# A hybrid decoder layer: the z product in token groups of 272/256/512 columns, splits moved from GpSimd to VectorE, and the residual's added row moved to w_out's token tiles

## The chip, the core and the metric

The kernel runs on one core of a Trainium2 chip. A core has five engines with queues of their own: TensorE (PE in the profile; PEld is its weight loads), VectorE (DVE), ScalarE (ACT), GpSimd (POOL) and SyncE (SP), which here only starts transfers. Each works through its queue in order. The metric is the device time of one execution in microseconds; the time of before is the median of three runs. A profile is of one more execution, whose span runs from its first to its last instruction.

## The reference

One layer over 1040 tokens (16 meta tokens and 1024 of the sequence), 1024 wide:

```
h = layer_norm(concat(meta, x), in_ln_g, in_ln_b)
z = h @ w_in + b_in                     # 3840 columns: q 512 | k 128 | v 128 | conv 2 x 512 | gates 2 x 1024
a = swa_sink_attention(q, k, v, ...)    # window 128, 16 meta keys, sinks, relative bias
c = silu(layer_norm(causal_dwconv(c_val * sigmoid(c_gate), 31 taps)))
mixed = sigmoid(g_attn) * (a @ w_attn_proj) + sigmoid(g_conv) * (c @ w_conv_proj)
h = layer_norm(alpha * h + mixed @ w_out)
f = (gelu(g) * u) @ ffn_w_down          # u, g = causal_dwconv(h @ ffn_w_up, 3 taps)
out = layer_norm(alpha * h + f)         # without the meta tokens
```

The first h, before the layer, is `xn * in_ln_g + in_ln_b` with xn the centred and scaled row. So the residual alpha * h is `xn * (alpha * in_ln_g) + alpha * in_ln_b`: a row that is multiplied and a row that is added.

## The kernel before

**Products.** Every large product is done with operands split in two: a float32 value is a high part (rounded by ACT, `nc.scalar.copy`) and a low part (the difference). A product of one 128-row chunk is three matmuls, high x high, high x low, low x high, the third with the low weights. `product` (line 297) issues them: lines 301, 305 and 306. The helper `split` (line 272) makes the two parts of a weight tile; its subtraction runs on DVE when `quick` is set and on POOL otherwise (line 276).

**Stages in order of time.** (1) The input stage to 56 us: rows of x are normed, transposed on PE, scaled and split into `h0`, the layer's input by channel, and the first tiles of z (k, v and q's first quarter) are formed at once, three tiles by three token groups `HG`, at lines 514 and 517. (2) The z product, to 416 us: 27 more tiles of 128 columns of `w_in` (8 of the convolution's input, 3 of q, 16 gates), each over all tokens. A tile is 8 chunks x 3 token groups x 3 matmuls, 72 in all. The conv tiles take the groups `ZG`, 400/384/256 columns, the q and gate tiles `TG`, the same without the first 14 tokens, 386/384/256. Attention (lines 740 to 873) runs in between, its matmuls among the gates'. DVE meanwhile runs the convolution, 31 taps for each of four channel chunks (line 669). Behind it, `csum` adds the four chunks for the LayerNorm over channels (lines 884 to 888), whose DVE work is pinned in order (`cln_*`), followed by the splits of attention's output (`o_split`, lines 985 to 991). (3) The projections of both branches, 416 to 505 us, eight tiles of `w_ab` (line 1079), merged with the gates that come back from DRAM (`merge`, line 1089). (4) w_out, 505 to 609 us, nine token tiles in the order 3, -1, 7, 2, 6, 0, 4, 1, 5 (`out_rows`, line 1228; -1 is the two meta rows that are kept). A tile loads its residual row from `h0d`, adds the product's two halves, norms and is transposed for the next stage during the next tile's product. (5) The up product with its convolution and gate, 609 to 1039 us (line 1497), and (6) the down product to the end (line 1635), both by a Strassen-like scheme of seven products on sums of quadrants.

**Where h0 lies.** Two buffers of 8320 columns, `RHO` and `RHC`, hold the eight chunks of h0, high and low. `h0(k, hl, a, b)` (line 255) gives columns a to b: part i = 2 (k mod 4) + hl begins at column 1040 i, so a matmul on the high part and the one on the low part read places 1040 columns apart. In the up product the quadrant sums (`bsum`, line 1154) lie four blocks of 256 or 258 columns apart, high to low, and one block from chunk to chunk; in the down product operands are blocks of 512 columns with the low part 1024 further.

**Weights.** `weights` (line 281) counts its calls: 1 to 3 are the input stage's, 4 to 30 z's, 31 to 38 the projections'. Up to the 23rd the split is on DVE, from the 24th on POOL. `pair_of` gives one of two buffers for each of the high and low parts; the low one begins 16 columns into its buffer.

**Evacuation.** A group's sum lies in one of three PSUM banks (`tag="mm", bufs=3`). ACT reads it into one of five buffers of 400 columns (`stage`, line 328). For a gate it is stored to `sgd` from ACT's queue (line 677); for q it is split and stored and loaded (`q_evac`).

**The residual** (line 438): the two rows of the input LayerNorm are loaded for all partitions, scaled by alpha, and DVE multiplies and adds them to the nine tiles of xn (line 450) behind the split of the fourth and the fifth weights; the result is stored to `h0d`.

**The order of work.** A planner orders each engine's instructions by rank (`rank`, a lower number first: `RK_TURN` 450, `RK_SPLIT` 500, `RK_EVAC` 600, and so on) and by its own timing. `after` pins one instruction behind another; in w_out, `line` (line 1166) makes one fixed order of DVE's work for tiles 0, 4, 1 and 5, in which the sums for the up product and the first splits of its weights stand between the tiles' own steps.

Of the kernel before, what the change touches and what calls it, by code (L numbers as in the profile page):

```python
# [29 lines left out]
P = 128  # L30
# [21 lines left out]

ZG = [(0, 400), (400, 784), (784, 1040)]

# [47 lines left out]
def tile_hybrid_layer(  # L102
# [152 lines left out]
    def h0(k, hl, a, b):  # L255
        o = ((k % 4) * 2 + hl) * T
        return (RHO if k < 4 else RHC)[:, o + a:o + b]
# [22 lines left out]

    def weights(shape, fill):
        fills[0] += 1
        n = fills[0]
        own = n == 3
        raw = sp.tile(shape, F, name="wr3") if own else wraw(shape)
        with rank({1: 13, 2: 18, 3: 17, 4: 23}.get(n, RK_SPLIT)):
            last_fill.append(fill(raw))
        hi, lo = (sp.tile(shape, R, name=t + "3") for t in ("whi", "wlo")) if own else pair_of("whi", "wlo", 16, shape)
        if n <= 3:
            return hi, lo, raw  # L290
        with rank(RK_SPLIT):
            last_split.append(split(raw, hi, lo, n <= 23))
        return hi, lo
# [31 lines left out]

    st_next = [0]

    def stage(n, lo=4104, cnt=5):
        i = st_next[0] % cnt
        st_next[0] += 1  # L330
        return FA[:, lo + i * 400:lo + i * 400 + n]

# [17 lines left out]
    def q_evac(r):  # L350
        def evac(g, a, b, ps):
            t = stage(b - a)
            nc.scalar.activation(t, ps, AF.Identity, bias=qb[:, r:r + 1], scale=HD ** -0.5)
            h, l = (qsp.tile([P, 400], R, name=n, tag=n)[:, :b - a] for n in ("qsh", "qsl"))
            nc.scalar.copy(h, t)
            nc.vector.tensor_tensor(l, t, f32(h), OP.subtract)
            for hl, (put, x) in enumerate(((store, f32(h)), (load, f32(l)))):
                c = 0
                if g == 0:
                    c = P + 2  # L360
                    put(qd[:, (hl * 4 + r) * c:(hl * 4 + r + 1) * c], x[:, :c])
                n = (b - a - c) // P
                if n == 0:
                    continue
                i = (a - U0 + c) // P
                put(dram(qd, q_at(i) + (hl * 4 + r) * P, [[8 * U, P], [8 * P, n], [1, P]]),
                    x[:, c:].rearrange("p (n q) -> p n q", q=P))
        return evac
# [69 lines left out]
    def residual(n, *js):  # L438

        if not gb:  # L440
            for i in range(2):
                gb.append(sp.tile([P, D], F, name="gb", tag="x", bufs=8))
                with rank(24):
                    load(gb[i], dram(ln0_in, i * D, [[0, P], [1, D]]))
            for t in gb:
                after(nc.vector.tensor_scalar(t, t, ALPHA, None, OP.mult), first_nm)
        for j in js:
            t, lo = (xns[j], 0) if j >= 0 else (xm, 96)
            for op, t2 in zip((OP.mult, OP.add), gb):
                after(nc.vector.tensor_tensor(t[lo:], t[lo:], t2[lo:], op), last_split[n])  # L450
            load(*((h0d[2 + j * P:2 + (j + 1) * P, :], t) if j >= 0 else (h0d[0:2, :], xm[96 + U0:96 + NMETA])))
# [171 lines left out]
    att = ExitStack()  # L623
    cp = att.enter_context(tc.tile_pool(name="cin", bufs=2, side="right", reuse_waits="tile"))
    ap = att.enter_context(tc.tile_pool(name="att", bufs=1, side="right", reuse_waits="tile"))

# [115 lines left out]
    gate_tile(0)  # L742
    ahead = chunks_done[first_chunk + KC + 5]

# [132 lines left out]
    for o in order:  # L877
# [4 lines left out]
        if o == "c3":  # L882

            csum = cp.tile([P, 16 + T], F, name="csum", tag="cin")[:, :U]
            with rank(RK_EVAC):
                nc.gpsimd.tensor_tensor(csum, acc[0], acc[1], OP.add)
                nc.gpsimd.tensor_tensor(csum, csum, acc[2], OP.add)
                nc.vector.tensor_tensor(csum, csum, acc[3], OP.add)
# [127 lines left out]
    for g in range(3):  # L1016
# [7 lines left out]
    wo_stack = ExitStack()  # L1024
    RW = wo_stack.enter_context(tc.tile_pool(name="rw", bufs=1, side="right", reuse_waits="tile")).tile(
        [P, 2048], R, name="RW")
    RT = OB[:, 0:2048]
# [50 lines left out]
    for m in range(KC):  # L1078
        hi, lo = weights([P, KC, P], lambda raw: load(raw, w_ab[m]))

# [32 lines left out]
        else:  # L1113
            pa = [branch(0, g, "mm", 3) if g < 3 else branch(0, g, "s", 2) for g in range(4)]
            for g in range(4):
                last_gate, last_act = merge(g, pa[g], branch(1, g, "t", 2))
        if m in (2, 3):
            raw = (FA[:, 4112:5136], OB[:, 3072:4096])[m - 2]
# [109 lines left out]
    def out_rows(i, between=(), work=()):  # L1228
# [13 lines left out]
        st = small.tile([P, 2, 6], F, name="st")  # L1242
        pin = line if i in (0, 4, 1, 5) else lambda ins: ins
        for half in range(2):
            hs = slice(half * 512, half * 512 + 512)
# [19 lines left out]
        if n < P:  # L1265
            q = FA[:4, 0:1024]
            load(q[0:2], h0d[0:2, :])
            nc.vector.tensor_tensor(r, r, q[0:2], OP.add)
            load(q[0:2], whole[2:4])
            nc.vector.tensor_tensor(r, r, q[0:2], OP.add)  # L1270
# [519 lines left out]
```

## Time and profile before

| what | us |
|---|---|
| median of three runs (1259.07 to 1259.88) | 1259.1 |
| the profiled execution's own time | 1259.33 |
| its span | 1257.1 |
| DVE L450, the residual's 18 multiplications and additions | 21.2 |
| POOL L276, all 19 splits on POOL | 47.5 |
| POOL L886 and L887, the two adds of csum | 4.0 |
| matmuls of z on PE by line and half (L301, L305, L306; `RHO`, `RHC`), six groups of 324 | 103.4 to 104.7 each, busy |

PE's granted clock was 0.998 of full speed. A row of a group view reads: line, engine, operation, output <- inputs, shape and count, then busy time and the mean of one in ns, then how long the engine sat idle before them and what ended it. A row of the timeline reads: start, duration (both us), engine, line, operation, operands, count; in brackets, the idle time before it and what released it. Matmuls are pipelined, so their durations overlap and the distance of their starts is what they cost. A row of the windows reads: the stretch, its length, and for each engine its busy time and count.

### The profile page before, as it was taken

The numbers are of one execution on the slowest core, as the hardware profiler recorded it, in microseconds if no ns is written. First come the engines' busy times: TensorE is split into PE (matmuls) and PEld (weight loads), VectorE is DVE, ScalarE is ACT, GpSimd is POOL, SyncE is SP. The second block draws the span as 40 slices with busy tenths as digits, with TensorE's granted clock in tenths as the row PEclk, the third lists the DMA queues.
The fourth block names the chain that finished last, engine by engine and source line by source line (L and its number), as shares of the span: only waits on it lengthen the run. The fifth ranks groups of instructions, "written<-read, shape, count | busy, mean of one in ns | idle before, by whom it ended". The sixth has DMA issues, their size and how long they took to land.

```text
span 1257.1 us, 21713 instructions
## 1 busy us (share of the span) xinstructions
PE 1246.0 (99%) x8546; PEld 1179.2 (94%) x8546; DVE 1086.6 (86%) x1859; ACT 587.4 (47%) x1057; POOL 54.1 (4%) x28
## 2 busy tenths in 40 slices
PE   9999999999999999999999999999999999999997
PEld 8999999999999999788899999999999998888886
DVE  7899989999989587648899999999999986995697
ACT  7522244545474222335565555554555554544330
POOL 0000000010112132000000000000000000000000
PEclk9999999999999999999999999999999999999999
DMA  7294733332155565222145555463464568998722
GB/s 279 73 309 104 192 95 97 106 94 81 68 141 178 155 171 140 77 75 101 68 134 185 193 210 187 184 218 117 154 230 164 203 211 318 390 328 298 249 86 84
DMA packets 96152, 212.10 MB, mean 169 GB/s; under 512 B 10787, under 2 KB 35939, under 8 KB 95922
## 3 DMA queue, kind: packets, MB, share of 16 engines
q1 hardware_dynamic: 84282, 199.64, 47.4%
q10 hardware_dynamic: 11768, 11.08, 2.7%
q8 instruction: 67, 1.10, 0.4%
q14 instruction: 35, 0.29, 0.1%
HBM read 150.29 MB, written 62.70 MB: 169 GB/s over the span
## 4 chain that ended last, share of the span: by engine, by line
PE 96%; ACT 1%; DVE 1%; DMA 0%; issue 0%; ACTq 0%; DVEq 0%; SPq 0%
PE px L1497 14%; PE py L1497 9%; PE ps_x L1635 9%; PE ps_z L305 8%; PE ps_z L301 8%; PE ps_z L306 8%; PE ps_z L1635 7%; PE pz L1497 5%; PE pw L1497 5%; PE ps_p L306 2%; PE ps_p L301 2%; PE ps_p L305 2%; PE ps_w L306 2%; PE ps_w L301 2%; PE ps_w L305 2%; PE ps_z L517 2%
## 5 line engine op out<-in xcount | busy, mean ns | idle before, releaser
L669 DVE SCALAR_TENSOR_TENSOR FA<-cin,cols,FA 128x1026 f32<-128x1026 f32 x120 | 155.2, 1305 | 0.2
L301 PE MATMUL ps_z<-RHO,whi 128*128 128x384 f32 (+2 forms) x324 | 104.7, 323 | 0.2 <-ACT FA L676 0.2
L305 PE MATMUL ps_z<-RHC,whi 128*128 128x384 f32 (+2 forms) x324 | 104.5, 323 | 0.0
L305 PE MATMUL ps_z<-RHO,whi 128*128 128x384 f32 (+2 forms) x324 | 104.0, 321 | 0.0
L306 PE MATMUL ps_z<-RHC,wlo 128*128 128x384 f32 (+2 forms) x324 | 103.7, 320 | 0.0
L301 PE MATMUL ps_z<-RHC,whi 128*128 128x384 f32 (+2 forms) x324 | 103.7, 320 | 0.0
L306 PE MATMUL ps_z<-RHO,wlo 128*128 128x384 f32 (+2 forms) x324 | 103.4, 319 | 0.0
L1316 DVE TENSOR_TENSOR RHO<-wr,RHO 128x512 fp32r<-128x512 f32 x94 | 63.6, 686 | 5.4 <-ACT RHO L1315 5.4
L1315 ACT CAST RHO<-wr 128x512 fp32r<-128x512 f32 x94 | 56.7, 620 | 24.4 <-DVE wr L1333 11.5
L273 ACT CAST whi<-wr 128x1024 fp32r<-128x1024 f32 x37 | 38.9, 1051 | 56.3 <-PE ps_z L305 31.9
L301 PEld LDWEIGHTS ps_z<-RHO,whi 128*128 128x128 f32 x324 | 60.9, 188 | 0.9 <-ACT FA L676 0.4
L305 PEld LDWEIGHTS ps_z<-RHC,whi 128*128 128x128 f32 x324 | 60.9, 188 | 0.4
L306 PEld LDWEIGHTS ps_z<-RHC,wlo 128*128 128x128 f32 x324 | 60.9, 188 | 0.2
L301 PEld LDWEIGHTS ps_z<-RHC,whi 128*128 128x128 f32 x324 | 60.9, 188 | 0.2
L306 PEld LDWEIGHTS ps_z<-RHO,wlo 128*128 128x128 f32 x324 | 61.0, 188 | 0.1
L305 PEld LDWEIGHTS ps_z<-RHO,whi 128*128 128x128 f32 x324 | 60.9, 188 | 0.1
L1333 DVE TENSOR_TENSOR wr<-wr 128x512 f32<-128x512 f32 x88 | 60.3, 685 | 0.2
L276 POOL TENSOR_TENSOR wlo<-wr,whi 128x1024 fp32r<-128x1024 f32 x17 | 42.3, 2488 | 185.3 <-ACT whi L273 175.7
L676 ACT ACTIVATE FA<-ps_z,cols 128x386 f32<-128x386 f32 (+2 forms) x48 | 26.0, 541 | 46.6 <-PE ps_z L306 39.1
L1509 ACT COPY FA<-px 128x514 f32<-128x514 f32 (+2 forms) x23 | 13.1, 571 | 68.0 <-PE px L1497 67.8
L1316 DVE TENSOR_TENSOR ws<-wr,ws 128x512 fp32r<-128x512 f32 x60 | 40.6, 686 | 4.5 <-ACT ws L1315 4.3
L1422 ACT ACTIVATE FA<-OB,cols 128x512 f32<-128x512 f32 x44 | 35.9, 816 | 14.0 <-DVE OB L1505 14.0
(467 smaller groups left out, 3567.3 us busy)
## 6 DMA issues: line engine op xcount, KB each, us to landing
wr<-in_w_up_dram SPq DMA_DIRECT2D x44, 512.0 KB, 4.6
wr<-in_w_z_dram SPq DMA_DIRECT2D x30, 512.0 KB, 4.0
fd<-FA SPq DMA_DIRECT2D x44, 256.0 KB, 2.5
OB<-in_w_down_dram SPq DMA_DIRECT2D x19, 512.0 KB, 6.2
qt<-qd SPq DMA_DIRECT2D x28, 256.0 KB, 3.7
td<-OB SPq DMA_DIRECT2D x12, 512.0 KB
sums<-fd SPq DMA_DIRECT2D x12, 512.0 KB, 4.8
sd<-sums SPq DMA_DIRECT2D x12, 512.0 KB, 2.7
```

The costliest lines, as they stand in the source:

```text
L273: ins = nc.scalar.copy(hi, raw)
L276: return (nc.vector if quick else nc.gpsimd).tensor_tensor(lo, raw, f32(hi), OP.subtract)
L301: ins = nc.tensor.matmul(ps, ah, bh, start=i == 0, stop=False)
L305: nc.tensor.matmul(ps, ah, bl, start=False, stop=False)
L306: last = nc.tensor.matmul(ps, al, bh, start=False, stop=i == n - 1)
L669: nc.vector.scalar_tensor_tensor(acc[c], cin[:, j:j + U], wc, acc[c], OP.mult, OP.add)
L1315: nc.scalar.copy(hi, src)
L1316: ins = nc.vector.tensor_tensor(lo, src, f32(hi), OP.subtract)
L1333: ins = nc.vector.tensor_tensor(*x)
L1422: nc.scalar.activation(t, cc[:, 2:HW], AF.Identity, bias=ffw(3, o), scale=ffw(2, o))
L1497: ins = nc.tensor.matmul(o, x[:, ks], bmat(sub, q, hl, k), start=first and k + j == 0, stop=k == 3 and j == 2, skip_group_check=not first)
L1635: nc.tensor.matmul(banks[i], l[:, ts], r[:, ws], start=first and a and x + k == 0, stop=z and x == len(ops) - 1 and k == 2, skip_group_che ...
```

## The change

Four edits are made together.

1. The token groups of z become 272/256/512 (258/256/512 for q and gates). h0's parts are laid out anew: the first 272 columns of the parts lie 272 columns apart behind column 6144 (those of the first part at 0), the other 768 columns lie 768 apart from column 272 on. The evacuation buffers become three of 272 and two of 512 columns. The anchor behind which attention begins, a chunk of the first gate tile, moves with the groups.
2. Where `weights` splits, the subtraction is always on DVE; csum's first two adds are on DVE. The splits of w_out's fourth to seventh chunk stay on POOL.
3. The low weights' offset of 16 columns is kept for the projections alone; z's begin at 0.
4. The residual stage only multiplies. The added row, alpha * in_ln_b, is loaded during the second tile of the projections, scaled by alpha at the fourth, and added to each tile of w_out before its product. A small pad moves attention's tiles by 8 columns.

```diff
-ZG = [(0, 400), (400, 784), (784, 1040)]
+ZG = [(0, 272), (272, 528), (528, 1040)]
...
     def h0(k, hl, a, b):
-        o = ((k % 4) * 2 + hl) * T
+        i = (k % 4) * 2 + hl
+        if a < 272:
+            o = i * 272 + (6144 if i else 0)
+        else:
+            o = i * 768
         return (RHO if k < 4 else RHC)[:, o + a:o + b]
...
-    def weights(shape, fill):
+    def weights(shape, fill, shift=0):
...
-        hi, lo = (...) if own else pair_of("whi", "wlo", 16, shape)
+        hi, lo = (...) if own else pair_of("whi", "wlo", shift, shape)
         if n <= 3:
             return hi, lo, raw
         with rank(RK_SPLIT):
-            last_split.append(split(raw, hi, lo, n <= 23))
+            last_split.append(split(raw, hi, lo, True))
...
-    st_next = [0]
-
-    def stage(n, lo=4104, cnt=5):
-        i = st_next[0] % cnt
-        st_next[0] += 1
-        return FA[:, lo + i * 400:lo + i * 400 + n]
+    st_next = [0, 0]
+
+    def stage(n):
+        big = n > 272
+        i = st_next[big] % (2 if big else 3)
+        st_next[big] += 1
+        o = 4136 + (816 + i * 512 if big else i * 272)
+        return FA[:, o:o + n]
...
         if not gb:
-            for i in range(2):
-                gb.append(sp.tile([P, D], F, name="gb", tag="x", bufs=8))
-                with rank(24):
-                    load(gb[i], dram(ln0_in, i * D, [[0, P], [1, D]]))
+            gb.append(sp.tile([P, D], F, name="gb", tag="x", bufs=8))
+            with rank(24):
+                load(gb[0], dram(ln0_in, 0, [[0, P], [1, D]]))
...
-            for op, t2 in zip((OP.mult, OP.add), gb):
-                after(nc.vector.tensor_tensor(t[lo:], t[lo:], t2[lo:], op), last_split[n])
+            after(nc.vector.tensor_tensor(t[lo:], t[lo:], gb[0][lo:], OP.mult), last_split[n])
...
+    cp.tile([P, 8], F, name="pad_i", tag="pad", bufs=1)
...
-    ahead = chunks_done[first_chunk + KC + 5]
+    ahead = chunks_done[first_chunk + 2 * KC + 2]
...
-                nc.gpsimd.tensor_tensor(csum, acc[0], acc[1], OP.add)
-                nc.gpsimd.tensor_tensor(csum, csum, acc[2], OP.add)
+                nc.vector.tensor_tensor(csum, acc[0], acc[1], OP.add)
+                nc.vector.tensor_tensor(csum, csum, acc[2], OP.add)
...
+    beta = rw_p.tile([P, D], F, name="beta")
...
-        hi, lo = weights([P, KC, P], lambda raw: load(raw, w_ab[m]))
+        hi, lo = weights([P, KC, P], lambda raw: load(raw, w_ab[m]), 16)
...
+        if m == 1:
+            load(beta, dram(ln0_in, D, [[0, P], [1, D]]))
+        if m == 3:
+            with rank(RK_EVAC):
+                nc.vector.tensor_scalar(beta, beta, ALPHA, None, OP.mult)
...
         pin = line if i in (0, 4, 1, 5) else lambda ins: ins
+        if n == P:
+            with rank(RK_TURN):
+                pin(nc.vector.tensor_tensor(r, r, beta, OP.add))
...
             nc.vector.tensor_tensor(r, r, q[0:2], OP.add)
+            nc.vector.tensor_tensor(r, r, beta[0:2], OP.add)
```

More of the change, by code (lines that the diff above doesn't have):

```diff
@@ L287, in weights @@
             last_fill.append(fill(raw))
-        hi, lo = (sp.tile(shape, R, name=t + "3") for t in ("whi", "wlo")) if own else pair_of("whi", "wlo", 16, shape)
+        hi, lo = (sp.tile(shape, R, name=t + "3") for t in ("whi", "wlo")) if own else pair_of("whi", "wlo", shift, shape)
         if n <= 3:
@@ L353, in evac @@
             nc.scalar.activation(t, ps, AF.Identity, bias=qb[:, r:r + 1], scale=HD ** -0.5)
-            h, l = (qsp.tile([P, 400], R, name=n, tag=n)[:, :b - a] for n in ("qsh", "qsl"))
+            h, l = (qsp.tile([P, 512], R, name=n, tag=n)[:, :b - a] for n in ("qsh", "qsl"))
             nc.scalar.copy(h, t)
@@ L1024, in tile_hybrid_layer @@
     wo_stack = ExitStack()
[L1025 to L1026 removed]
+    rw_p = wo_stack.enter_context(tc.tile_pool(name="rw", bufs=1, side="right", reuse_waits="tile"))
+    RW = rw_p.tile([P, 2048], R, name="RW")
+    beta = rw_p.tile([P, D], F, name="beta")
     RT = OB[:, 0:2048]
```

## The prediction

> **What bounds the kernel now.** I read the page's busy times first, then the waits of TensorE, then its timeline.
>
> ```profile
> span 1257.1 us, 21713 instructions
> PE 1246.0 (99%) x8546; PEld 1179.2 (94%) x8546; DVE 1086.6 (86%) x1859; ACT 587.4 (47%) x1057; POOL 54.1 (4%) x28
> ```
>
> TensorE (PE) has work in 1246.0 of 1257.1 us. Who it waited for, from the view of its waits (us in total, times, longest):
>
> ```profile
> PE ps_w L541 <- DVE ones_r L222: 1.1, 1, 1.1
> PE pw L1497 <- ACT FA L1298: 1.0, 1, 1.0
> PE ps_z L301 <- ACT FA L676: 0.2, 1, 0.2
> ```
>
> These are the two longest, and the only one in the z product behind the input stage. So no edit can gain much by ending a wait; time falls only if PE's matmuls stand closer together, and rises if a slower engine makes PE wait. How close they stand is read from starts in the timeline (start, us, engine, line), not from durations, because matmuls overlap. The rows that begin each group of 24 matmuls, for one tile of the convolution's input (groups 400/384/256) and one gate tile (386/384/256), with the first row behind:
>
> ```profile
> 67.89 0.34 PE L301 MATMUL ps_z<-RHO,whi 128*128 128x400 f32 x1
> 72.23 0.34 PE L301 MATMUL ps_z<-RHO,whi 128*128 128x384 f32 x1
> 76.45 0.28 PE L301 MATMUL ps_z<-RHO,whi 128*128 128x256 f32 x1
> 79.28 0.34 PE L301 MATMUL ps_z<-RHO,whi 128*128 128x400 f32 x1
> ...
> 405.17 0.34 PE L301 MATMUL ps_z<-RHO,whi 128*128 128x386 f32 x1
> 409.44 0.34 PE L301 MATMUL ps_z<-RHO,whi 128*128 128x384 f32 x1
> 413.65 0.28 PE L301 MATMUL ps_z<-RHO,whi 128*128 128x256 f32 x1
> 416.48 0.28 PE L301 MATMUL ps_p<-OA,whi 128*128 128x258 f32 x1
> ```
>
> The conv tile takes 11.39 us, the gate tile 11.31: per matmul 181 ns at 400 columns, 178 at 386, 175 at 384, 118 at 256. Other stages show what a matmul can cost:
>
> ```profile
> 609.05 1.58 PE L1497 MATMUL px<-OC,RHO 128*128 128x256 f32 x12
> 610.46 1.58 PE L1497 MATMUL pz<-OC,RHO 128*128 128x256 f32 x12
> ...
> 631.95 1.60 PE L1497 MATMUL px<-RHC,ws 128*128 128x258 f32 x12
> 633.39 1.52 PE L1497 MATMUL px<-OC,ws 128*128 128x256 f32 x12
> 634.75 1.59 PE L1497 MATMUL pz<-RHO 128*128 128x258 f32 x12
> ...
> 1044.95 5.60 PE L1635 MATMUL ps_z<-OC,RX 128*128 128x512 f32 x24
> 1050.39 5.60 PE L1635 MATMUL ps_z<-OC,RHC 128*128 128x512 f32 x24
> ```
>
> 512 columns: 5.44 us for 24, 226.7 ns each. 256 columns at 633.39: 1.36 us for 12, 113.3 ns, the same 0.443 ns per column. 258 columns: 120 ns, some 5.6 more than 0.443 x 258. At 0.443 the z groups would be 177, 171, 170 and 113.4: each stands 4 to 7 ns too far apart. In the code the operands of the rows without this extra follow each other in steps of whole 256 columns (256 and 1024 in the up product, 512 and 1024 in the last one); with it are steps of 258 there and of 1040 in z. The row at 609.05 speaks against the step as the only cause: the same 256-column operands, 117.5 ns.
>
> **The change part by part.**
>
> *The z groups.* The columns and the matmuls stay (27 tiles of 72 on this path). The 256 and 512 groups now read parts 768 columns apart, three times 256; the first group, 258 or 272, reads parts 272 apart. A gate or q tile (19 of them) becomes 24 x (120 + 113.3 + 226.7) = 11.04 us, against 11.31: 0.27 less. If 256 stays at 117.5, it is 11.14: 0.17 less. 272 has no clean row; 120 x 272/258 = 126.5 makes a conv tile (8) 11.20 to 11.30 against 11.39: 0.19 to 0.09 less. Sum: 19 x 0.27 + 8 x 0.19 = 6.6 us, or 19 x 0.17 + 8 x 0.09 = 3.9. I take 6.2, near the upper figure, since the 256 group follows a 258 or 272 group, as at 633.39; a part of the tiles is cut up by attention and counts for less. Lower end: the extra belongs to every matmul in z whatever its step; three per term then stay three, gain 0. Upper end: 258 and 272 lose theirs too, 24 x 5.6 ns x 27 = 3.6 more, gain 10.2.
>
> [...]
>
> *The low weights lie 16 columns lower.* Nothing is issued for it. The up product's weights have no such shift and run at 113.3, so 0; if the shift was worth 5 ns to the third that reads the low weights, 648 x 5 ns = 3.2 us are lost.
>
> *The evacuation's buffers* become three of 272 columns and two of 512 instead of five of 400. A gate tile's results leave them by a store, for which ACT has waited:
>
> ```profile
> ACT FA L676 <- DMA sgd<-FA: 6.3, 2, 3.3
> ```
>
> A buffer came round after 5/3 of a tile; now a small one after 1.5 tiles, a large one after two, so these waits may grow by a us or two. Behind ACT queue the next evacuations, and for these PE waits only when its three banks, a whole tile of 11 us, are full: 0. The anchor that lets attention begin moves from the 14th to the 19th of the first gate tile's 24 chunks, which is 66% and 69% of its columns: 0.
>
> *The input stage* writes to the same new places, its groups of 384 included:
>
> ```profile
> 27.17 9.47 PE ps_z L517 x54
> ```
>
> 175.4 ns each, in the chain of waits; at 170.0 the stage's 144 such matmuls give 0.8 us. Matmuls here also follow DVE's and ACT's parts, so I take 0.4 (0 to 0.8).
>
> *GpSimd's splits on VectorE (DVE).* Rows by line, and DVE beside a GpSimd (POOL) split:
>
> ```profile
> L276 POOL TENSOR_TENSOR wlo<-wr,whi 128x1024 fp32r<-128x1024 f32 x17 | 42.3, 2488 | 185.3 <-ACT whi L273 175.7 <-PE ps_m L891 9.6
> L276 DVE TENSOR_TENSOR wlo<-wr,whi 128x1024 fp32r<-128x1024 f32 x20 | 24.2, 1211 | 1.3 <-ACT whi L273 1.3
> ...
> 376.14 2.65 POOL L276 TENSOR_TENSOR wlo<-wr,whi 128x1024 fp32r<-128x1024 f32 x1 [13.63 <-ACT whi L273]
> ...
> 375.50 0.35 DVE L977 CAST OC<-FA 128x386 fp32r<-128x386 f32 x1
> 376.44 2.57 DVE L977 CAST OC<-FA 128x386 fp32r<-128x386 f32 x1
> ...
> 278.95 2.00 POOL L886 TENSOR_TENSOR csum<-FA 128x1026 f32<-128x1026 f32 x1 [275.64 <-DVE FA L669]
> 344.31 1.23 DVE L888 TENSOR_TENSOR csum<-csum,FA 128x1026 f32<-128x1026 f32 x1
> ```
>
> Fifteen of the 17 move (the tiles' 24th to 38th weights); two of w_out's stay. Each took 2.5 us of POOL and held DVE: the cast at 376.44 took 2.57 instead of 0.35. On DVE it is 1.21, about 1 us less of DVE's time than the hold. Two adds of csum move too, 2 x 1.23. PE gains nothing, as it didn't wait for DVE here; the windows (PE, PEld, DVE, ACT, POOL busy) show DVE's room:
>
> ```profile
> 145.00:350.00 205.00, 205.00 (x1350) 200.41 (x1351) 194.25 (x392) 100.85 (x261) 11.25 (x5) 1.00 0.33 96
> 350.00:417.00 67.00, 66.79 (x430) 66.39 (x429) 59.11 (x112) 37.23 (x58) 13.48 (x6) 1.00 0.62 175
> 579.00:609.00 30.00, 30.00 (x146) 25.10 (x145) 25.41 (x41) 17.10 (x38) 0.00 (x0) 1.00 0.21 77
> ```
>
> *The added row.*
>
> ```profile
> L450 DVE TENSOR_TENSOR xn<-xn,gb 128x1024 f32<-128x1024 f32 x8 | 9.4, 1214 | 0.0
> L450 DVE TENSOR_TENSOR OB<-OB,gb 128x1024 f32<-128x1024 f32 x8 | 9.4, 1206 | 0.0
> ```
>
> Half of these (and one of the two on the meta rows) go, some 10.9 us of DVE behind the input stage, worth nothing to PE, which doesn't wait there; DVE starts the convolutions earlier. One row load and its scaling move to the projections, on SP's queue ahead of gate loads and under PE's work. Eight adds of 1.21 us come into w_out's tiles. They need only the stored row, so the product covers them, except at the end, where three (tiles 4, 1 and 5) stand in DVE's fixed order between 579 and 609:
>
> ```profile
> 607.18 0.69 DVE L1197 TENSOR_TENSOR FA<-OB,FA 128x520 f32<-128x520 f32 x1
> 609.25 0.69 DVE L1251 TENSOR_TENSOR OB<-ps_w,OB 128x512 f32<-128x512 f32 x1 [1.38 <-PE ps_w L306]
> 615.49 1.68 PE L1497 MATMUL pw<-RHC,RHO 128*128 128x256 f32 x12 [0.98 <-ACT FA L1298]
> ```
>
> DVE waits 1.38 us for w_out's last product; from there to 615.49 the chain is the norm, the transposes and ACT, and PE already waits for it. DVE has 30 - 25.41 = 4.6 us free in that window and gets 3 x 1.21 = 3.6. If it can use all its gaps, PE loses 0; if only the last, 3.6 - 1.4 = 2.2. I take 0.5.
>
> **Sum.** Against the profiled execution's own 1259.33 us (span 1257.1 and 2.2 around it): -6.2 - 0.4 + 0.5 = -6.1, so 1253.2. That execution lies 0.2 above the median of the runs, 1259.1, so I say 1253.0.
>
> **The rivals.**
>
> *No gain in z.* The extra follows the stage, not the step or the width. For it: the row at 609.05, where operands in whole steps of 256 columns still took 117.5. Against it: the 512 groups stand 226.7 apart, without any extra. The time is 1259.1 + 0.5 - 0.4 = 1259.2. [...]
>
> *The end of w_out.* The three adds find no gaps, and 256 stays at 117.5: 1259.1 - 3.9 + 2.2 = 1257.4; with the 113.3 it is 1254.7.
>
> *Slower: a split holds DVE's queue.* A split on DVE needs ACT's high half, which waits until PE gives a buffer free: POOL stood 175.7 us for it. If DVE stands there in POOL's place, the conv LayerNorm and the splits of attention's output queue behind it, and the projections wait for them.
>
> ```profile
> 399.33 0.56 DVE L991 TENSOR_TENSOR OA<-OB,OA 128x386 fp32r<-128x386 f32 x1
> ```
>
> This is the last piece that the projections' first group needs, ready at 399.9; PE would come at 416.48 - 6.6 = 409.9, so 10 us are spare. Eight POOL splits lie before that, each holding DVE some 2.2 us today, so it decides from (10 + 17.6)/8 = 3.5 us a split, 2.3 of them waiting. At 5 us it costs 8 x 5 - 17.6 - 10 = 12.4: 1265.4. Against it: the 20 splits already on DVE waited 1.3 us in all.
>
> **Chances and range.** Forecast 0.60 (own range 1250.5 to 1255.5: more or less of the 256 term, the low weights, the end of w_out). The end of w_out 0.16, of which 0.12 at 1254.7 and 0.04 at 1257.4. No gain in z 0.13. Slower 0.11. A measurement of this kernel tells 0.2%, 2.5 us, from no change. Faster holds the forecast and the better case of w_out's end: 0.72; within 0.2% no gain in z and the worse one: 0.17; slower: 0.11. The range 1249.4 to 1260.0 takes in the forecast, its upper gain almost, and the two rivals without a loss; it leaves out the slower case and little else.
>
> **What would show it.** Right: a gate tile's groups start about 2.9, 2.7 and 5.4 us apart, 11.04 in all, and the projections begin 6 to 7 us sooner; DVE's splits wait next to nothing for ACT; the cast at L977 is 0.35 each time; the wait of pw at L1497 is 1.0 to 1.5 us. Wrong: 512 groups in z at 231 ns or more; PE waiting for DVE or ACT between 145 and 420 us; the wait at L1497 over 3 us.

## The result: 1261.7 us against 1259.6, and the profile after

The changed kernel takes 1261.67 us (median; 1260.12 to 1264.28), the kernel before 1259.61 beside it (1259.07 to 1260.01): a ratio of 1.0019, 95% interval [1.0013, 1.0026]. It is slower by 0.2%. The prediction, 1253.0 with a range up to 1260.0, was wrong in sign. The runs of the new kernel also spread over 4 us, those of the old one over 1. They fall into two groups by the mean clock that PE was granted in each run: nine runs at 0.998 or 0.999 have a median of 1261.2, eight at 0.995 to 0.997 one of 1262.9. The kernel before shows 0.998 or 0.999 wherever the clock of a run is on record.

The page's first lines of the changed kernel, and from the view of TensorE's waits the longest, the one at the start of the up product and two short new ones (us in total, times, longest):

```profile
span 1260.1 us, 21710 instructions
PE 1246.7 (99%) x8546; PEld 1152.2 (91%) x8546; DVE 1081.0 (86%) x1876; ACT 586.2 (47%) x1056; POOL 12.3 (1%) x11
```

```profile
PE ps_s L838 <- DMA qt<-qd: 1.6, 1, 1.6
...
PE pw L1512 <- ACT FA L1313: 0.8, 1, 0.8
...
PE ps_h L1300 <- DVE OB L1290: 0.2, 1, 0.2
PE pz L1300 <- DVE FA L1520: 0.2, 1, 0.2
```

PE is busy 99% as before. New are a wait of 1.6 us for a DMA, the load of q for attention's first scores, and short waits for DVE in transposes (ps_h, pz). Where the 3.1 us between the two spans arose, by the starts of each stage's first matmul in the two timelines (us):

| stretch | before | after | difference |
|---|---|---|---|
| to the z product | 56.38 | 56.47 | +0.09 |
| z product and attention | 360.10 | 361.95 | +1.85 |
| projections | 88.00 | 88.00 | 0 |
| w_out | 104.57 | 105.05 | +0.48 |
| entry to the up product (609.05 to 631.95) | 22.90 | 23.54 | +0.64 |
| the rest | 625.11 | 625.11 | 0 |

The stage that was to give 6.2 us lost 1.85. Three things are in this number. The first is the distance of the matmuls. A gate tile's groups in the timeline (start, duration, engine, line), with the first row of the projections:

```profile
395.96 0.28 PE L305 MATMUL ps_z<-RHO,whi 128*128 128x258 f32 x1
...
398.86 0.28 PE L305 MATMUL ps_z<-RHO,whi 128*128 128x256 f32 x1
...
401.69 0.40 PE L305 MATMUL ps_z<-RHO,whi 128*128 128x512 f32 x1
...
407.19 0.28 PE L305 MATMUL ps_z<-RHO,whi 128*128 128x258 f32 x1
...
418.42 0.28 PE L305 MATMUL ps_p<-OA,whi 128*128 128x258 f32 x1
```

24 matmuls take 2.90, 2.83 and 5.50 us: 121, 118 and 229 ns each, 11.23 us for the tile. Before it was 11.31, predicted 11.04. Over nineteen tiles that would be 1.5 us, not 5.1. The first four conv tiles, with the few matmuls of others that stand among them, take 46.20 us against 46.61: in two of them the 256 group takes 113.4 ns a matmul, in the other two 118.

The second is the wait at the start of attention, and the third stands behind it. The windows show the granted clock (the number ahead of the last two):

```profile
139.10 0.28 PE L310 MATMUL ps_z<-RHC,wlo 128*128 128x258 f32 x1
140.97 0.31 PE L838 MATMUL ps_s<-kx,qt 128*128 128x144 f32 x1 [1.59 <-DMA qt<-qd]
```

```profile
139.10:140.90 1.80, 0.28 (x3) 0.07 (x1) 1.80 (x3) 0.48 (x1) 0.00 (x0) 1.00 0.90 216
...
141.90:145.20 3.30, 3.30 (x17) 3.30 (x17) 3.30 (x8) 0.00 (x0) 0.00 (x0) 0.50 1.01 275
```

PE stands from 139.1 to 141.0, 1.75 us more than from one matmul to the next, and then runs at a clock of 0.50 for 3.3 us: half of those, 1.6 us, is lost as well (the 24 matmuls of 256 columns that begin at 141.44 stand 184 ns apart instead of 118). As z is 1.85 us longer in all, its groups gain some 1.5 us, and the wait with its clock takes 3.35.

Why is the load late? The chain of waits, followed back from there (start, us, what):

```profile
127.40 4.50 DMA qd<-qsh
132.00 0.42 ACT qsh L361
132.44 2.87 DMA qd<-qsh
135.35 0.47 SPq L113
135.88 4.96 DMA qt<-qd
140.97 0.31 PE ps_s L838
```

A part of q is stored (4.50 us), which frees the buffer for the next part; that one is stored (2.87) and the load takes another 4.96. It is hardly later than it was. SP began to issue these loads at 135.35; before it was 135.07, and there the typical load landed 6.6 us behind its issue (SP's timeline and the page's DMA issues in that stretch):

```profile
135.07 2.41 SPq L113 DMA_DIRECT2D qt<-qd  x4
```

```profile
qt<-qd SPq DMA_DIRECT2D x4, 260.0 KB, 6.6
```

```profile
136.91 0.34 PE L301 MATMUL ps_z<-RHO,whi 128*128 128x386 f32 x1
...
141.89 0.23 PE L833 MATMUL ps_s<-kx,qt 128*128 128x144 f32 x1
```

All these are rows of before: PE asked for q at 141.89, 4.98 us into the first gate tile, behind its group of 386 columns and four more matmuls; 135.07 + 6.6 is 141.7, just in time by this estimate. In the changed kernel the planner again puts the first scores behind the first group. That group is now 258 columns wide, so PE asks at 139.2, 2.9 us into the tile that begins at 136.33. The need moved, not the load.

The end of w_out, on VectorE in the changed kernel:

```profile
608.57 1.22 DVE L1257 TENSOR_TENSOR OB<-OB,beta 128x1024 f32<-128x1024 f32 x1
609.89 0.69 DVE L1265 TENSOR_TENSOR OB<-ps_w,OB 128x512 f32<-128x512 f32 x1
...
612.44 0.68 DVE L1265 TENSOR_TENSOR OB<-ps_w,OB 128x512 f32<-128x512 f32 x1
```

Before, DVE stood idle for 1.38 us and then took the last half of w_out as soon as PE had it. Now the row's add for tile 5 fills this gap and no idle time is left ahead of the last half: PE begins its last matmul there at 611.24, and DVE takes the sum at 612.44, 1.20 us later. Before, the two stood 0.43 apart (608.82 and 609.25).

### The profile page after: what moved, and what is told of

Its sections match the earlier page's. It is cut to its first block, busy times and chain, and to the rows that moved or that the text cites. A ratio compares the mean times of both kernels' runs of the same rounds, so it can differ in the third digit from the quotient of the medians.

```text
span 1260.1 us, 21710 instructions
## 1 busy us (share of the span) xinstructions
PE 1246.7 (99%) x8546; PEld 1152.2 (91%) x8546; DVE 1081.0 (86%) x1876; ACT 586.2 (47%) x1056; POOL 12.3 (1%) x11
## 4 chain that ended last, share of the span: by engine, by line
PE 94%; DVE 3%; DMA 1%; ACT 1%; issue 0%; SPq 0%; DVEq 0%; ACTq 0%
PE px L1512 14%; PE py L1512 10%; PE ps_x L1650 9%; PE ps_z L309 8%; PE ps_z L305 8%; PE ps_z L310 8%; PE ps_z L1650 7%; PE pz L1512 5%; PE pw L1512 5%; PE ps_p L310 2%; PE ps_p L305 2%; PE ps_p L309 2%; PE ps_z L521 2%; PE ps_w L310 1%; PE ps_w L305 1%; PE ps_w L309 1%
## 5 line engine op out<-in xcount | busy, mean ns | idle before, releaser
L309 PE MATMUL ps_z<-RHO,whi 128*128 128x256 f32 (+2 forms) x324 | 104.7, 323 | 0.0
L305 PE MATMUL ps_z<-RHO,whi 128*128 128x256 f32 (+2 forms) x324 | 104.4, 322 | 0.0
L310 PE MATMUL ps_z<-RHC,wlo 128*128 128x256 f32 (+2 forms) x324 | 104.2, 322 | 0.0
L310 PE MATMUL ps_z<-RHO,wlo 128*128 128x256 f32 (+2 forms) x324 | 104.1, 321 | 0.0
L305 PE MATMUL ps_z<-RHC,whi 128*128 128x256 f32 (+2 forms) x324 | 104.0, 321 | 0.0
L309 PE MATMUL ps_z<-RHC,whi 128*128 128x256 f32 (+2 forms) x324 | 103.8, 321 | 0.0
L280 DVE TENSOR_TENSOR wlo<-wr,whi 128x1024 fp32r<-128x1024 f32 x35 | 42.7, 1221 | 8.1 <-ACT whi L277 7.3
L681 ACT ACTIVATE FA<-ps_z,cols 128x258 f32<-128x258 f32 (+2 forms) x48 | 26.0, 542 | 39.0 <-PE ps_z L310 33.3
L1512 PE MATMUL px<-OA,RHO 128*128 128x258 f32 (+1 forms) x324 | 42.2, 279 | 0.0
```

What stands on the lines that cost most here:

```text
L280: return (nc.vector if quick else nc.gpsimd).tensor_tensor(lo, raw, f32(hi), OP.subtract)
L305: ins = nc.tensor.matmul(ps, ah, bh, start=i == 0, stop=False)
L309: nc.tensor.matmul(ps, ah, bl, start=False, stop=False)
L310: last = nc.tensor.matmul(ps, al, bh, start=False, stop=i == n - 1)
L681: nc.scalar.activation(t, ps, AF.Tanh, bias=bcol(14 + i), scale=0.5)
L1512: ins = nc.tensor.matmul(o, x[:, ks], bmat(sub, q, hl, k), start=first and k + j == 0, stop=k == 3 and j == 2, skip_group_check=not first)
```

## The experiments

Ratios are to the kernel before, run beside each; a line number belongs to the kernel named with it.

**The added row alone.** The kernel before, with part 4 of the change, without its small pad, and nothing else.

```diff
-            for op, t2 in zip((OP.mult, OP.add), gb): ...
+            after(nc.vector.tensor_tensor(t[lo:], t[lo:], gb[0][lo:], OP.mult), last_split[n])
...
+                pin(nc.vector.tensor_tensor(r, r, beta, OP.add))
```

> The kernel before with the residual's added row moved to w_out's tiles and nothing else. Theory of the three terms (the changed kernel's 2 to 3 us are a wait for q's load of 1.6 to 1.9 us, the added row with about 1.1 us at the end of w_out and the entry to the up product, and a z product that gains nothing): +1.1 us against before, the projections begin at 416.5 as before, and PE's extra stands behind 590 us, in the turn of tile 1, the last transposes and the first products of the up part. Rival (the added row is hidden, and the late microsecond comes from the other parts): 0.0 us.

Measured: 1261.81 us, 1.0020 [1.0011, 1.0029], so +2.4, more than either theory. The loss behind 590 us is there: from w_out's first matmul to the up product's first 258 group it is 118.21 us against 117.24, so 1.0 more. Another 1.2 us lie in attention, where before had no wait. One row of its waits, then the timeline of GpSimd and VectorE there:

```profile
PE ps_o L866 <- DVE OB L793: 1.0, 1, 1.0
```

```profile
335.65 2.64 POOL L276 TENSOR_TENSOR wlo<-wr,whi 128x1024 fp32r<-128x1024 f32 x1 [9.79 <-ACT whi L273]
...
336.07 3.31 DVE L667 SCALAR_TENSOR_TENSOR FA<-cin,cols,FA 128x1026 f32<-128x1026 f32 x1
...
339.41 0.69 DVE L793 TENSOR_TENSOR OB<-OB,ps_o 64x512 f32<-64x512 f32 x1
```

A tap of the convolution took 3.31 us instead of some 1.3 (the median of the seven from 329 to 340 is 1.287) while a GpSimd split ran, and attention's sum (L793), for which PE stood 1.0 us, was queued behind it. That DVE's queue stands otherwise here because it has ten us less to do behind the input stage is argued, not shown; the longer tap, and what was queued behind it, are in the rows. The split ends at 338.29 and the tap 1.1 us later, at 339.38. What makes the tap longer is not shown.

**Attention's first scores later.** The changed kernel with one pin more.

```diff
+                if i == g == r == 0:
+                    after(ins, chunks_done[first_chunk + 2 * KC])
```

> The changed kernel with attention's first score matmul pinned behind the first 512-column chunk of the first gate tile, some 3.6 us later on PE than the planner put it. Theory of the three terms: PE no longer waits for q's load, the projections begin about 1.7 us sooner than in the changed kernel (416.7 us), the time is 1.5 to 2 us less (about 1259.8), and the spread of the runs is smaller. Rival (the wait moves to the next late thing of attention): the wait of 1.6 us shows up again later in z, no gain.

Measured: 1259.27 us (1258.64 to 1260.86), 0.9999 [0.9990, 1.0008]: 2.4 us less than the changed kernel by the medians, with about half of its spread; only its longest run has a mean clock under 0.998. That is more than the wait, as the half clock went with it. The projections begin at 415.66. PE asks for q at 142.5 and doesn't wait; its windows show the clock at 1.00 throughout:

```profile
139.00:142.00 3.00, 3.00 (x28) 3.00 (x27) 3.00 (x4) 0.48 (x1) 0.00 (x0) 1.00 1.03 236
142.00:146.00 4.00, 3.94 (x36) 3.27 (x35) 4.00 (x8) 0.47 (x1) 0.00 (x0) 1.00 1.04 277
```

z now takes 358.95 us against 360.10 before, of which a new wait of 0.2 at 144.5 is to be taken off: the groups alone are worth some 1.4 us. The added row, 1.0 us in the same stretch behind z as above, takes most of it back.

**Where the operands lie.** The changed kernel with h0's parts 272 columns lower.

```diff
-            o = i * 272 + (6144 if i else 0)
+            o = i * 272 + (6144 if i >= 0 else 0)
...
-            o = i * 768
+            o = i * 768 + -272
```

> The changed kernel with all eight first groups of h0 behind column 6144, so that the 256 and 512 groups of every part begin 272 columns lower: their byte addresses are then 192 modulo 256 instead of 0, as are those of the products that run at 226.7 ns for 512 columns. Theory A (where the operands lie modulo 256 bytes sets the extra): 512 groups at 226.7 instead of 229.4 ns and 256 groups at 113.3 instead of 118; 27 tiles x 24 x (2.7 + 4.5) ns = 4.7 us less than the changed kernel, about 1257. Theory B (the extra is a state of PE that a group of matmuls falls into, whatever its addresses): 229 to 231 and 118 ns as in the changed kernel, no difference beyond 0.5 us.

Measured: 1261.88 us, 1.0021 [1.0011, 1.0030]: no gain. The distances did move with the place, 512 groups from 229.4 to 227.8 ns and 256 groups from 117.9 to 119.7, but against each other: 258, 256 and 512 together are 467.5 ns in both. (These are the gate tiles; the two conv tiles' groups at 113.4 went to 120.0.) That is Theory B in the time, while the place has an effect of its own. The profile holds another wait for q, of 2.3 us, and behind it the full clock:

```profile
142.80:146.20 3.40, 3.32 (x28) 3.35 (x29) 3.40 (x8) 0.00 (x0) 0.00 (x0) 1.00 1.07 280
```

**z's parts alone.** The changed kernel with GpSimd's splits, csum and the added row as before (and without the pad).

```diff
-            last_split.append(split(raw, hi, lo, True))
+            last_split.append(split(raw, hi, lo, n <= 23))
...
-                nc.vector.tensor_tensor(csum, acc[0], acc[1], OP.add)
+                nc.gpsimd.tensor_tensor(csum, acc[0], acc[1], OP.add)
...
-                pin(nc.vector.tensor_tensor(r, r, beta, OP.add))
```

> The changed kernel with its z groups, layout of h0, evacuation buffers, anchor and low weights, but GpSimd's splits, csum's adds and the residual's added row as before. Theory of the three terms: z's matmuls gain nothing, the wait for q's load stands (1.6 to 1.9 us), nothing is lost behind 590 us: +1.8 us against before, 1261. Rival 1 (the new groups do gain some us, and the splits on DVE give them back): 1253 to 1257. Rival 2 (the wait for q's load comes from DVE's new splits): no wait, 1259.3.

Measured: 1264.49 us, 1.0040 [1.0027, 1.0053], +5.1: worse than all four parts together. Three waits make it:

```profile
PE ps_z L305 <- ACT FA L682: 1.8, 1, 1.8
PE ps_s L839 <- DMA qt<-qd: 1.5, 1, 1.5
...
PE ps_o L874 <- DVE OB L801: 1.0, 1, 1.0
```

```profile
389.00 1.91 ACT L977 ACTIVATE FA<-FA,cols 128x384 f32<-128x384 f32 x3
390.82 1.03 ACT L277 CAST whi<-wr 128x1024 fp32r<-128x1024 f32 x1
391.75 0.68 ACT L682 ACTIVATE FA<-ps_z,cols 128x512 f32<-128x512 f32 x1
```

```profile
393.80:397.00 3.20, 3.20 (x9) 2.51 (x8) 3.10 (x7) 2.40 (x5) 0.50 (x1) 0.50 0.64 165
```

The load of q is late, as the theory of the three terms has it, here with the full clock behind it, and the third is an attention sum late on DVE once more. The first is new. An evacuation on ACT (L682, 391.75 in the timeline) stands behind the conv LayerNorm and a split's high half, PE waits 1.8 us for a bank, and the window behind it shows a clock of 0.50 for 3.2 us: another 1.6. The four, 5.9 us, less z's gain of 1.4 are 4.5 of the 5.1. So Rival 1 was right in this, that the splits on DVE matter to the whole, and wrong in its sign: they take waits away.

**The added row back.** The kernel of the second experiment with the row in the input stage.

```diff
-            after(nc.vector.tensor_tensor(t[lo:], t[lo:], gb[0][lo:], OP.mult), last_split[n])
+            for op, t2 in zip((OP.mult, OP.add), gb):
+                after(nc.vector.tensor_tensor(t[lo:], t[lo:], t2[lo:], op), last_split[n])
...
-                pin(nc.vector.tensor_tensor(r, r, beta, OP.add))
```

> The changed kernel with attention's first score matmul pinned as in e2_anchor and the residual's added row back in the input stage. Theory: the row costs 1.1 us at the end of w_out and the entry to the up product, and there alone, so 1.1 us less than e2_anchor (1258.2), 1.2 us less than before; the last half of w_out is again waited for by VectorE (some 1.4 us idle) and not the other way round. Rival (VectorE's 10 us more in the input stage make the convolutions late, and a wait comes up in attention): the same as e2_anchor or worse.

Measured: 1258.37 us, 0.9992 [0.9983, 1.0000], as expected. DVE waits for w_out's last half again:

```profile
608.56 0.69 DVE L1260 TENSOR_TENSOR OB<-ps_w,OB 128x512 f32<-128x512 f32 x1 [1.36 <-PE ps_w L310]
```

**The low weights' place.** The same with z's low weights 64 columns higher, and 16 columns higher as before the change.

```diff
-    def weights(shape, fill, shift=0):
+    def weights(shape, fill, shift=64):
```

> e5_anchor_row_back with z's low weights 64 columns higher. In the changed kernel the convolution's tiles alternate: 256 groups at 118.1 and 113.4 ns, 272 groups at 129.5 and 124.9, in step with the two weight buffers, whose low parts begin at byte addresses 448 and 192 modulo 512. Theory A (the place of the low weights modulo 512 sets which of the two a tile gets): the alternation turns round, 113.4 in the first and third clean conv tile and 118.1 in the second and fourth. Theory B (it is something else that alternates): as before the shift. Under both the time moves by less than 0.5 us.

> e5_anchor_row_back with z's low weights 16 columns higher, as they were before the change. The prediction's bound: worth 0 to 3.2 us of loss if taken away, so here a gain of up to 3.2 us; taken value 0. Theory (place of operands moves single groups by 1 to 5 ns, up and down): under 1 us either way, with the 256, 258 and 512 groups of the gate tiles within 3 ns of 117.9, 120.2 and 229.4.

Measured: 1258.70 and 1258.60 us; each profile has 0.8 us more of the wait for q's second load than the kernel they are compared with, so that the times say nothing under 0.5 us. With 16 columns the 512 groups stand at 230.3 or 228.9 ns, 256 at 117.8, 258 at 120.2: a ns up and down, the loss of 3.2 us that was bounded isn't there. With 64 columns the first and the third conv tile kept 118.1 ns in their 256 groups, where Theory A had 113.4. There is a stronger case against the place: in the kernel without the shift the planner laid two matmuls of another group into the second conv tile, and its 256 group took 118.1 ns where the kernel of the second experiment took 113.4, with the same operands at the same addresses. So the place alone doesn't decide; that the two matmuls do is argued, not shown.

**Splits back on GpSimd.** `e5_anchor_row_back` with part 2 undone; the diff is that of `e4_z_only` without its last line.

> e5_anchor_row_back with the weights' splits and csum's first adds on GpSimd again. Prediction's value: 0, since PE does not wait for VectorE. Theory from e1_row_only and e4_z_only: a split on GpSimd stretches a convolution tap on VectorE from 1.3 to 3.3 us, and where an attention step stands behind that tap PE waits about 1 us; and ScalarE's evacuations stand behind the conv LayerNorm near 390 us: 1 to 4 us more than e5_anchor_row_back. Rival (those waits were the planner's luck in e4_z_only and came with the late q load): no difference.

Measured: 1260.52 us, 1.0008 [0.9999, 1.0017], 2.15 more than with the splits on DVE. One wait explains 1.3 of it:

```profile
PE ps_o L877 <- DVE OB L802: 1.3, 1, 1.3
```

```profile
330.95 2.56 POOL L280 TENSOR_TENSOR wlo<-wr,whi 128x1024 fp32r<-128x1024 f32 x1 [12.12 <-ACT whi L277]
...
331.17 2.43 DVE L779 TENSOR_TENSOR pm<-s,pm 128x64 f32<-128x64 f32 x1
```

A subtraction of 64 columns, 0.22 us elsewhere, took 2.43 under GpSimd's split, and the sum of attention behind it came late. The wait for ACT of `e4_z_only` didn't come back.

**The meta queries later too.** `e5_anchor_row_back` with the anchor `ahead` at the first gate tile's last chunk.

```diff
-    ahead = chunks_done[first_chunk + 2 * KC + 2]
+    ahead = chunks_done[first_chunk + 3 * KC - 1]
```

> e5_anchor_row_back with the anchor of the two meta queries' score matmuls (one 2-column matmul for each head) moved from the 19th to the last of the first gate tile's 24 chunks, some 1.1 us later on PE. Theory: the wait there for q's second load (0.2 us in this kernel's profile, 1.0 us in those of e6_shift64 and e7_shift16) goes, 0.2 to 1.0 us less: about 1257.9, and less than before by more than the measurement is uncertain. Rival (the load is late by more than that, or attention's next step is then late): the same as e5_anchor_row_back.

Measured: 1258.22 us (1257.68 to 1258.53), 0.9988 [0.9979, 0.9997]: no wait for q is left, and the kernel is faster than before, by 0.12%.

**High and low parts 3072 columns apart.** The last kernel with h0 laid out anew.

```diff
-        i = (k % 4) * 2 + hl
+        i = hl * 4 + k % 4
...
-            o = i * 272 + (6144 if i else 0)
+            o = i * 272 + 6144
...
-            o = i * 768
+            o = i * 768 - 272
```

> e9_later with h0's parts in another order, the four high parts first and then the four low ones, and all first groups behind column 6144: a high part and its low part lie 3072 columns apart (a multiple of 1024, as in w_out and the down product) instead of 768, one chunk and the next still 768. Theory A (the distance of the operands that a chunk's three matmuls read sets the extra, the prediction's step theory in another form): 512 groups at 226.7 ns, 256 groups at 113.3, up to 4.7 us less than e9_later. Theory B (PE keeps a state, and the place of operands moves it by a ns or two only): 512 groups between 227.5 and 230.5, 256 between 117.5 and 120.5, the same time within 0.6 us.

Measured: 1257.69 us, 0.9986 [0.9977, 0.9995], the lowest of all, and below `e9_later` by no more than the two intervals leave open. A gate tile:

```profile
393.30 0.28 PE L305 MATMUL ps_z<-RHO,whi 128*128 128x258 f32 x1
...
396.17 0.28 PE L305 MATMUL ps_z<-RHO,whi 128*128 128x256 f32 x1
...
399.04 0.40 PE L305 MATMUL ps_z<-RHO,whi 128*128 128x512 f32 x1
...
404.50 0.28 PE L305 MATMUL ps_z<-RHO,whi 128*128 128x258 f32 x1
```

2.87, 2.87 and 5.46 us: some 119.5, 119.5 and 227.7 ns, not 113.3 and 226.7. Theory B.

**The splits alone.** The kernel before with part 2 of the change.

```diff
-            last_split.append(split(raw, hi, lo, n <= 23))
+            last_split.append(split(raw, hi, lo, True))
...
-                nc.gpsimd.tensor_tensor(csum, acc[0], acc[1], OP.add)
+                nc.vector.tensor_tensor(csum, acc[0], acc[1], OP.add)
```

> The kernel before with the weights' splits and csum's first adds on VectorE and nothing else. Prediction's value: 0, as PE waits for VectorE nowhere in z: 1259.4. Rival (what e8_pool shows holds here too: GpSimd's splits cost PE 1 to 2 us in attention): 1 to 2 us less; against it, before's profile has no such wait.

Measured: 1258.92 us, 0.9996 [0.9987, 1.0004]: 0.7 less, not told apart from nothing, nor from a gain of 1 us (the interval reaches to 1.6). The two profiles have the same span, 1257.1 us, and neither has a wait in attention. So the value 0 fits here. In `e8_pool` the same splits cost 2 us; that the other parts have set DVE's queue there so that a stretched operation meets attention is argued, not shown.

**A second profile of the changed kernel,** nothing edited.

> The changed kernel once more, for a second profile. Theory (the wait for q's load is there each time, and half the clock behind it only in some executions): a wait of 1 to 2.5 us at the first score matmul; with the clock at 0.5 behind it for some 3.4 us the projections begin at 418.4 and the 24 matmuls of 256 columns that follow stand 184 ns apart, without it at about 416.8 and 118 ns. Rival (the half clock belongs to the kernel): it is there again at the same place.

Measured: 1262.81 us in its one run. The wait is there, longer, and so is the half clock behind it:

```profile
PE ps_s L838 <- DMA qt<-qd: 2.1, 1, 2.1
```

```profile
142.80:146.10 3.30, 3.30 (x18) 3.30 (x17) 3.30 (x7) 0.00 (x0) 0.00 (x0) 0.51 1.06 281
```

Both profiles of this kernel have it; that of `e3_phase`, with the longer wait of 2.3, doesn't. The clocks of the single runs say more. By estimate one such stretch lowers the mean clock of a run by 0.0013 (half of 3.3 us in 1260), and of the 17 runs of the result only eight are that low. So it comes in about half of the executions, as the theory has it, and those take 1.8 us more by the medians. That it lies at this place in the runs without a profile is not shown.

**What sets 113 or 118.** `e9_later` with whole first groups, and with the gate tiles' groups turned round.

```diff
+        c = 0 if a == U0 else a
...
-        product(ps[:, :b - a], [(hi[:, k], lo[:, k], h0(k, 0, a, b), h0(k, 1, a, b)) for k in range(KC)])
+        product(ps[:, :b - c], [(hi[:, k], lo[:, k], h0(k, 0, c, b), h0(k, 1, c, b)) for k in range(KC)])
...
-            evac(g, a, b, ps[:, :b - a])
+            evac(g, a, b, ps[:, a - c:b - c])
```

```diff
-        for g, (a, b) in enumerate(groups):
+        for g, (a, b) in list(enumerate(groups))[::-1 if evac.__name__ == "gate_evac" else 1]:
```

> e9_later with the first group of the q and gate tiles made over columns 0 to 272 instead of 14 to 272; the 14 columns more are not read. Theory A (a group whose operands begin off a multiple of 16 columns sets PE's slow state, and the groups behind inherit it): 272 groups at 124.9 ns as in the conv tiles of the changed kernel, the 256 groups behind them at 113.4 and the 512 groups at 229 or less, no loss of time in spite of 14 columns more. Theory B (the start column has nothing to do with it): 272 at 125 to 130, 256 at 118, 512 at 229.4; 19 tiles x 24 x (125.4 - 120.5) ns = 2.2 us more than e9_later.

> e9_later with the gate tiles' groups in the order 512, 256, 258. Theory A (a 256 group takes its distance over from the group ahead): behind a 512 group it moves off 117.9 ns, to 113.4 if the 512 group leaves the fast state. Theory B (the distance belongs to the z operands): 117.9, 120.2 to 120.5 and 229.4 in any order. The time by the distances alone: the same as e9_later within 0.5 us under B, up to 16 tiles x 24 x 4.5 ns = 1.7 us less under A; the score matmuls of attention meet other chunks, which may add a wait.

Measured, whole groups: 1259.88 us, 1.0003 [0.9994, 1.0013], 1.7 more than `e9_later`. Two q tiles, one after the other:

```profile
103.25 0.29 PE L305 MATMUL ps_z<-RHO,whi 128*128 128x272 f32 x1
...
106.24 0.28 PE L305 MATMUL ps_z<-RHO,whi 128*128 128x256 f32 x1
...
108.97 0.39 PE L305 MATMUL ps_z<-RHO,whi 128*128 128x512 f32 x1
...
114.46 0.29 PE L305 MATMUL ps_z<-RHO,whi 128*128 128x272 f32 x1
...
117.47 0.29 PE L305 MATMUL ps_z<-RHO,whi 128*128 128x256 f32 x1
...
120.30 0.40 PE L305 MATMUL ps_z<-RHO,whi 128*128 128x512 f32 x1
```

The first tile's 256 group takes 2.73 us (113.4 ns a matmul, mean of its 24), the second's 2.83 (118.1), and the next two tiles repeat this; the 272 groups ahead of them take 124.8 and 125.4. Behind a 258 group that begins at column 14 no 256 group of a q or gate tile ran at 113. Groups turned round: 1260.26 us, 1.0008 [0.9998, 1.0018]; behind a 512 group two of four clean 256 groups ran at 113.3 ns, the others at 117.8. So the Theory A of each is half right: a 256 group of these two kernels took one of two distances (113.3 to 113.4 or 117.8 to 118.1 ns), and which one changed with the groups ahead of it. The two weight buffers, which the tiles use in turns, don't decide it alone: the 26th of the 27 tiles reads the same buffer as the 6th (the second of the two above), but its 256 group (398.02 to 400.74) runs at 113.4 ns. What sets the distance stays open, and so does why z's 512 groups never reached 226.7. (The second kernel is no faster for it: its profile has a wait of 2.2 us for an evacuation on ACT, as in `e4_z_only`.)

## Why the prediction was wrong

**The z groups: the step that failed first.** "The 256 and 512 groups now read parts 768 columns apart, three times 256" took 113.3 and 226.7 ns from other stages, on the theory that the step between operands makes the extra. Three layouts (768 apart, the same 272 columns lower, 3072 apart) gave 117.9 to 120 and 227.8 to 229.4, but for two conv tiles at 113.4 in the first. The term measured 1.4 us, not 6.2; of the 8.7 us between forecast and median, 4.8 are this term's. The row at 609.05, quoted there as speaking against the step, was the one to believe; "No gain in z" was the rival that came nearest. Its 1259.2 is also what the second experiment measured (1259.27), but by luck: there a gain of 1.4 in z and a loss of 1.0 at the end of w_out nearly cancel, where the rival had 0 and 0.5, and 0.4 less in the input stage. None of the three signs of being wrong came (512 groups at 231 ns, PE waiting for DVE or ACT between 145 and 420 us, over 3 us at the up product's start); they watched other places than those that failed.

**The anchor: "0".** The step looked at the anchor written in the code, 66% and 69% of a tile, and took it for the one behind which attention begins. It holds only the meta queries' matmuls. The first scores have no anchor; the planner puts them behind the first group, and that shrank by a third. It costs 1.75 us and, in both profiles of this kernel and by their clocks in about half of its runs, 1.6 more. No rival had a wait for a load. The profile of before showed how little was spare: 141.7 against 141.89.

**The end of w_out: right mechanism, wrong size.** 0.5 taken, 1.1 measured (0.48 + 0.64), inside its bounds of 0 to 2.2. DVE's 4.6 us of free time in that window couldn't all be used: the last gap was.

**The input stage.** 0.4 less expected; z begins 0.09 later. The 384 groups there didn't come closer either.

**The splits.** 0 fits the kernel before (`e11_splits_only`), and its sub-steps hold: 35 splits at 1.22 us, and the cast that had taken 2.57 is 0.35 each time:

```profile
L280 DVE TENSOR_TENSOR wlo<-wr,whi x35: 1203/1220/1228, 52.2 to 487.8; 128x1024 fp32r<-128x1024 f32 x35
...
L982 DVE CAST OC<-FA x8: 351/354/358, 384.6 to 395.7; 128x386 fp32r<-128x386 f32 x4, 128x384 fp32r<-128x384 f32 x4
```

But it isn't 0 beside the other parts: there GpSimd's splits cost 2 us, so this part kept the change from being worse. The slower rival, a split that holds DVE's queue, shows nowhere: no wait of PE leads to a split, and DVE's 35 splits waited 8.1 us in all, some 0.2 each. (The rival counted eight of GpSimd's splits before 399.9; there were seven, as the eighth began at 406.43, which makes its limit 3.6 us a split instead of 3.5.) The low weights' 0 holds too, by `e7_shift16`. The evacuation's 0 holds in the changed kernel, but not in general: in `e4_z_only` and `e14_order` PE did wait 1.8 and 2.2 us for it.

**The sum by its own terms.** From 1259.6, the median of before beside it: 1259.6 - 1.4 + 0.1 + 1.1 = 1259.4. With the wait it is 1261.2, and with the half clock as well 1262.8. The two groups of runs have medians of 1261.2 and 1262.9, so the terms account for both.

## What to carry to other kernels

A matmul's distance in one stage is no price for another stage, not even at equal width (256 columns: 113.3 ns at 633.39 in the up product, 117.9 in z's gate tiles); if one row of the same width contradicts the theory, take the stage's own distance. When groups become smaller, look at everything the scheduler places "behind the first group": it moves earlier (here from 141.89 to 139.2 us), and what it needs doesn't (the load's issue began at 135.07, then at 135.35). On PE, 99% busy here, a wait of 1.75 us cost 3.35 in the changed kernel's profile, as 1.6 more were lost at half the clock behind it, though not in every execution. And where the runs of a kernel spread, look at the clock of each run before giving one number to the loss.

## What the runs showed of the hardware

Behind a wait of 1.6 us PE's clock was 0.50 from 141.83 to 145.24 in the changed kernel, 3.41 us. It was 0.51 for 3.3 us behind a wait of 2.1 (`e12_again`) and 0.50 for 3.2 us behind one of 1.8 (`e4_z_only`), while behind others of 1.5 (`e4_z_only`), 2.2 (`e14_order`) and 2.3 us (`e3_phase`) it stayed at 1.00. So the wait's length alone doesn't decide whether the clock falls; what does is not shown.

In the changed kernel a 256 group of z that ran at the full clock, with no other matmuls among its own, stood at one of two distances: 113.3 ns a matmul in the second and fourth conv tile, 117.9 in the first and in the q and gate tiles, as means of whole groups of 24. The same operands ran at either (the second conv tile, 113.4 in `e2_anchor`, 118.1 in `e5_anchor_row_back`). With the operands 272 columns lower the gate tiles' 256 groups went from 117.9 to 119.7 ns and the 512 groups from 229.4 to 227.8 (`e3_phase`).

A VectorE operation beside a GpSimd split took some 2 us more in these rows: 3.31 instead of 1.3 us for a tap (`e1_row_only`), 2.43 instead of 0.22 for a subtraction of 64 columns (`e8_pool`).
